# Rounded queries times key-value matrices, and three reordered steps, in a gated-linear and latent-attention block

## The chip, the cores and the metric

The kernel runs on one core of one Trainium2 chip. The metric is the device time of a whole execution in microseconds; lower is better. Times are medians of several executions, and one further execution is taken by the hardware profiler, whose rows are quoted here.

The core's engines run side by side, each with its own queue of instructions: TensorE (PE; its weight loads are listed as PEld), VectorE (DVE), ScalarE (ACT), GpSimd (POOL) and SyncE (SP), which here only issues transfers. They wait for each other through semaphores. TensorE accumulates into PSUM banks; all other working data lies in SBUF.

## The reference

One block on 512 tokens of width 1024, batch 1, in float32: an RMS norm, one wide input projection, two branches, a gated merge, an output projection, and an MLP with squared ReLU. Cut to what the change touches:

```python
def gla_direction(q, k, v, log_a, include_diag):       # per head; DK = 128, DV = 256
    b = jnp.cumsum(log_a, axis=3)
    q_dec = q * jnp.exp(b)
    k_dec = k * jnp.exp(-b)
    k_end = k * jnp.exp(b_last - b)
    scores = jnp.where(mask, einsum(q_dec, k_dec), 0.0)
    o_intra = einsum(scores, v)
    # over chunks:
    o = einsum('bhck,bhkv->bhcv', qc, state)
    state = state * dc[..., None] + einsum('bhck,bhcv->bhkv', kc, vc)

o = rmsnorm(o_f + o_b, g_gla) * silu(gr)               # four heads, forward and backward

q = rmsnorm(cq, g_q) @ w_uq                            # eight heads of the second branch
kv = rmsnorm(ckv, g_kv) @ w_ukv
k_rope = rope(kr, positions)                           # one rotary key for all heads
p = softmax(q k^T);  y_mla = p v

merged = sigmoid(z_ma) * y_gla + sigmoid(z_mb) * y_mla
h = h + merged @ w_out
h = h + square(relu(rmsnorm(h) @ w_ff1)) @ w_ff2
out = rmsnorm(h, g_final)
```

The gated-linear branch carries a key-value matrix, the state, of 128 by 256 for each head and direction. The kernel is free to choose how it chunks the sequence.

## The kernel before, in words

**Arithmetic.** Most float32 products are made of three rounded ones. A tensor x is kept as a pair: hi is x in the type fp32r (ScalarE writes it, `split`, L93), lo is x - hi, also in fp32r (a subtraction, L94, on VectorE, or on GpSimd where `split` is given that engine; `split_scaled`, L97 and L98, does the same with a factor). `mm3` (L87 to L90) then issues three matmuls into one accumulator: hi by hi (L88), hi by lo (L89), lo by hi (L90). Weights are loaded by SyncE into a staging tile and split; their tiles end in f, h and l (`gk2f`, `gk2h`, `gk2l`). Where both operands are left in plain float32, there is one `nc.tensor.matmul`, which the trace lists as two instructions.

**Stages.** (1) The input projection: blocks of it as one level of a seven-product scheme, the rest as 128 columns at a time against the split, transposed input `xT`. (2) The four heads of the gated-linear branch, from about 180 to 290 us, with the remaining input projections in between to fill TensorE. (3) The eight heads of the second branch ("the attention"), from about 296 us, as scores, softmax, transposes and values, with the up-projections of later heads and the first output-projection products in between. (4) The output projection and the MLP, in the seven-product scheme again.

**A head of the gated-linear branch**, in the loop of L1257 for heads 0 to 2 and written out from L1305 for the last. The 512 tokens are four blocks of 128, the state is taken over halves of 256. `Gates(h + 1)` (L441) makes the next head's decays: Abs, Exp and Ln on ScalarE (`logs`, L460), scans and differences on VectorE (`sums`, L463 to L476), exponentials (`exps`). `Scaled` multiplies queries and keys by them; `across` leaves in `far` (`qk3`) the queries (`far[:, 0]`) and keys (`far[:, 1]`) scaled to reach the other half of the sequence. `gla_scores` (L540) makes the scores inside a half (`sc`, split) and turns the far keys (`kT`, split). `gla_state` (L574) multiplies these by the values `v`, 24 rounded matmuls of 256 columns into one bank, and copies the bank to `gla{h}s`. `gla_out` (L727) accumulates into two banks: scores by values, 24 rounded matmuls, and then the far queries by the state of the other half, four plain float32 matmuls (L742). `gla_squares` and `gla_gated` (L763) norm and gate the result out of those two banks. Between state and output stand the weights' low part of the next projection (`lows`, L243) and other splits on VectorE.

**Around the last head.** Names that the steps touch: `rotary.tables` (L858; sine and cosine on ScalarE), `rotary_k` (L891 to L897; writes `krsin`, `kswap` and `kr` on VectorE), `ckv_.diagonals` (L811; the reciprocal norm of the key latent as a split diagonal `ckvdg`, L292) and `ckv_.spread` (L818, matmuls on L301 that spread it over the partitions), `rotary_begin` (L864; weights `wr0`, `wr1`) and `up_T` with them (`ro`), `rotary_q` (L878), `rotary_k_split` (`kbuf`), the gates `zb4` to `zb7` (`over_rms`, L375, then Tanh), and `up_units(0)`, the first pair of attention heads: queries `uq`, keys `uk`, values `uv`. `zb7` is the last projection before the attention; its weights are begun at L1330, its products run at L1338.

**Banks.** PSUM has eight banks in two rings of four: the tag "mm" (projections) and the tag "at" (scores, states, outputs, transposes). `ps(tag, name)` takes the next bank of its ring, and its first write waits until the bank's previous reader is done. `proj_begin(w, col, name, tag="mm")` (L231) loads, splits and takes a bank.

**Order.** Instructions of an engine keep the order in which they were issued. A scheduler may move them where the program doesn't fix it: `in_program_order(start, engines)` (L110) pins the named engines' order for the instructions since a mark, and `goes_behind` (L125) puts one group behind another. GpSimd is pinned to the program's order over all four heads (L1343), TensorE is up to L1341 (`ordered`, from the input projection on), and the attention is left to the scheduler but for the groups that `goes_behind` names.

Of the kernel before, what the change touches and what calls it, by code (L numbers as in the profile page):

```python
# [14 lines left out]
AF = mybir.ActivationFunctionType  # L15
# [3 lines left out]
P = 128  # L19
# [6 lines left out]
GH, GDV = 4, 256  # L26
# [9 lines left out]
C_ZA, C_ZB = 3776, 4800  # L36
# [20 lines left out]
def tile_block(ctx: ExitStack, tc: tile.TileContext, t, out: bass.AP):  # L57
    nc = tc.nc
# [5 lines left out]
    def tl(shape, dt, tag, bufs, name):  # L64
        serial[0] += 1
        return sb.tile(shape, dt, tag=tag, bufs=bufs, name=f"{name}_{serial[0]}")

    def u2(name, dt=F32, shape=(P, S)):
        return tl(list(shape), dt, "u2", 29, name)

    def u4(name, dt=F32R, shape=(P, 2, S)):
        return tl(list(shape), dt, "u4", 26, name)
# [14 lines left out]
    def mm3(acc, lh, ll, rh, rl, start, stop, onto=False):  # L87
        nc.tensor.matmul(acc, lh, rh, start=start, stop=False, skip_group_check=onto)  # L88
        nc.tensor.matmul(acc, lh, rl, start=False, stop=False, skip_group_check=onto)  # L89
        nc.tensor.matmul(acc, ll, rh, start=False, stop=stop, skip_group_check=onto)  # L90

    def split(hi, lo, src, rest=nc.vector):
        nc.scalar.activation(hi, src, AF.Copy)  # L93
        rest.tensor_tensor(lo, src, raw(hi), op=ALU.subtract)  # L94
# [134 lines left out]
    w_in = t["w_in"][0]  # L229

    def proj_begin(w, col, name, tag="mm"):  # L231
        wh, wl = weights(w[:, col : col + P], name)
        return wh, wl, ps(tag, name)
# [139 lines left out]
    def over_rms(acc, name):  # L373
        z = u2(f"z{name}")
        nc.vector.tensor_tensor(z, acc, R, op=ALU.mult)  # L375
        return z
# [163 lines left out]
    def gla_scores(near, nxt, far):  # L540


        bd = ps("at", "bd")
        for j in range(NT):
            nc.tensor.matmul(  # L545
                bd[:, j * P : (j + 1) * P], near["b"][:, 1, j], near["b"][:, 0, j], start=True, stop=True
            )
        scs = [ps("at", f"sc{g}") for g in range(2)]

        def block(j, i):  # L550
            at = (j % 2) * 256 + (i % 2) * P
            return scs[j // 2][:, at : at + P]

        for j in range(NT):
            n = j + 1 if j % 2 == 0 else j - 1
            nc.tensor.matmul(block(j, j), near["f"][:, 1, j], near["f"][:, 0, j], start=True, stop=True)
            nc.tensor.matmul(block(j, n), nxt[:, 1, j], nxt[:, 0, n], start=True, stop=True)
        kt = ps("at", "kt")
        for j in range(NT):
            nc.tensor.transpose(kt[:, j * P : (j + 1) * P], far[:, 1, j], ident)  # L560
        bds = u2("bds")
        nc.scalar.activation(bds, bd, AF.Copy)  # L562
        res = [u4(f"sc{g}") for g in range(2)]
        for g in range(2):
            for j in (2 * g, 2 * g + 1):
                nc.vector.copy_predicated(block(j, j), after.bitcast(I32), bds[:, j * P : (j + 1) * P])
            nc.scalar.activation(res[g][:, 0, :], scs[g], AF.Copy)
        for g in range(2):
            nc.vector.tensor_tensor(res[g][:, 1, :], scs[g], raw(res[g][:, 0, :]), op=ALU.subtract)
        keys = u4("kT")  # L570
        split(keys[:, 0, :], keys[:, 1, :], kt)
        return res, keys, far

    def gla_state(h, keys):  # L574

        half, at = h // 2, (h % 2) * GDV
        c = slice(at, at + GDV)
        acc = ps("at", f"gla{h}st")
        for j in range(NT):
            tok = slice(j * P, (j + 1) * P)  # L580
            mm3(acc[:, (j // 2) * GDV : (j // 2 + 1) * GDV], keys[:, 0, tok], keys[:, 1, tok],
                v[j, half][:, 0, c], v[j, half][:, 1, c], j % 2 == 0, j % 2 == 1)
        state = u2(f"gla{h}s")
        nc.scalar.activation(state, acc, AF.Copy)
        return state

# [138 lines left out]
    def gla_out(h, sc, state, far):  # L727

        half, at = h // 2, (h % 2) * GDV
        accs = [ps("at", f"gla{h}o{g}") for g in range(2)]  # L730
        c = slice(at, at + GDV)
        os = [accs[i // 2][:, (i % 2) * GDV : (i % 2 + 1) * GDV] for i in range(NT)]
        for i, o in enumerate(os):
            g = i // 2
            for x in range(2):
                j = 2 * g + x
                tok = slice(x * 256 + (i % 2) * P, x * 256 + (i % 2 + 1) * P)
                mm3(o, sc[g][:, 0, tok], sc[g][:, 1, tok], v[j, half][:, 0, c], v[j, half][:, 1, c],
                    i % 2 == 0 and x == 0, False, True)
        for i, o in enumerate(os):  # L740
            other = 1 - i // 2
            nc.tensor.matmul(  # L742
                o, far[:, 0, i], state[:, other * GDV : (other + 1) * GDV], start=False, stop=True,
                skip_group_check=True,
            )
        return os

    def gla_squares(h, os):
# [31 lines left out]
    class Latent:  # L780
# [4 lines left out]
        def begin(self, j):  # L785
            self.begun[j] = proj_begin(w_in, self.col + j * P, f"{self.name}{j}")
# [104 lines left out]
    def rotary_k():  # L891
        r = slice(64, 96)
        sgn = u2("krsin")
        nc.vector.tensor_scalar(sgn[r], sin[r], cst[r, K_SIGN : K_SIGN + 1], None, op0=ALU.mult)
        nc.vector.tensor_tensor(kswap[r], kswap[r], sgn[r], op=ALU.mult)
        nc.vector.tensor_tensor(kr[r], kr[r], cos[r], op=ALU.mult)
        nc.vector.tensor_tensor(kr[r], kr[r], kswap[r], op=ALU.add)  # L897
# [285 lines left out]
    ckv_, cq_ = Latent(C_CKV, 2, V_KV, "ckv"), Latent(C_CQ, 3, V_Q, "cq")  # L1183
# [7 lines left out]
    for n, (a, m) in enumerate(steps[:-4]):  # L1191
# [4 lines left out]
        if steps[n + 1] in fillers:  # L1196
            at = traced()
# [57 lines left out]
    rotary = Rotary()  # L1255
    pooled = traced()
    for h in range(GH - 1):  # L1257
        sc, keys, far = gla_scores(*scaled_qk.parts())
        scaled_qk = Scaled(h + 1)
        gate = Gates(h + 1)  # L1260
        gate.logs()
        latent, j = ((cq_, 1), (cq_, 2), (ckv_, 0))[h]
        acc = latent.products(j)
        if h < 2:
            w_b, lows = begin_late(C_GQ + (h + 2) * P, f"gq{h + 2}")
        else:
            ckv_.begun[1], lows = begin_late(C_CKV + P, "ckv1")
        (rotary.angles, rotary.reduced, cq_.diagonals)[h]()
        gate.sums("f")
        state = gla_state(h, keys)  # L1270
        gate.exps("f")
        lows()
        latent.keep(j, acc)
        gate.sums("b")
        gate.exps("b")
        scaled_qk.within("f", gate.parts)
        scaled_qk.across("f", gate.parts)
        if j:
            latent.add_squares()
        if h:  # L1280
            gla_turn(h - 1)
        os = gla_out(h, sc, state, far)
        scaled_qk.within("b", gate.parts)
        rs = gla_squares(h, os)
        scaled_qk.across("b", gate.parts)
        if h < 2:
            w_k = begin_qk(h + 2, 1)
            gla_gated(h, os, rs)
            finish_qk(h + 2, 0, w_b)
            if h == 0:  # L1290
                cq_.begin(2)
            else:
                ckv_.begin(0)
                cq_.sums()
            finish_qk(h + 2, 1, w_k)
        else:
            zb = begin(C_ZB + 4 * P, "zb4")
            gla_gated(h, os, rs)
            cq_.spread()
            ckv_.keep(1, ckv_.products(1))  # L1300
            ckv_.add_squares()
            w_b = begin(C_ZB + 5 * P, "zb5")
            zb = proj_run(zb, xT)

    h = GH - 1  # L1305
    sc, keys, far = gla_scores(*scaled_qk.parts())
    ckv_.sums()
    zb5 = proj_run(w_b, xT)
    cq = cq_.normed()
    state = gla_state(h, keys)  # L1310
    cos, sin = rotary.tables()
    late = [over_rms(acc, f"b{f}") for f, acc in ((4, zb), (5, zb5))]
    rotary_k()
    ckv_.diagonals()
    wr = rotary_begin()
    zb = begin(C_ZB + 6 * P, "zb6")
    kbuf = rotary_k_split()
# [9 lines left out]
    ro = rotary_q(accs)  # L1327
    zb = over_rms(proj_run(zb, xT), "b6")
    next(units)
    w_b = begin(C_ZB + 7 * P, "zb7")  # L1330
    g2.append(half_tanh(zb, "b6"))
    first_units = traced()
    for n, _ in enumerate(units):
# [3 lines left out]
    at = traced()  # L1337
# [20 lines left out]
    at = traced()  # L1358
# [4 lines left out]
    for n in range(4 * MH + LAG_C - 1):  # L1363
# [12 lines left out]
        if 2 <= n % 8 < 7:  # L1376
            at = traced()
# [5 lines left out]
        if n in (6, 14):  # L1383
            units = up_units(n // 8 + 2)
            at = traced()
# [3 lines left out]
        b = n - LAG_B  # L1389
        if n == 30:  # L1390
            xs_ = wo_accs[1] = [ps("mm", f"wox{rb}") for rb in range(2)]
            at = traced()
# [13 lines left out]
        for x, at in (("y", (18, 26, 34)), ("z", (20, 28, 36))):  # L1406
            if n in at:
                p = at.index(n)
                to = (5, 6) if x == "y" else (7, 3)
                split_sum(wo_left[p], sums_of[p, x], *to, f"{x}o{p}", nc.gpsimd if p < 2 else nc.vector)  # L1410
        if n in (19, 30):
            p = (19, 30).index(n)
# [12 lines left out]
        if n == 17:  # L1425
            at = traced()
# [235 lines left out]
    at = traced()  # L1662
# [9 lines left out]
    at = traced()  # L1672
# [7 lines left out]
    at = traced()  # L1680
# [12 lines left out]
    at = traced()  # L1693
# [8 lines left out]
    for qd in range(NQ):  # L1702
# [14 lines left out]
        for n, m in enumerate(ORDER):  # L1717
# [4 lines left out]
            if m == 2:  # L1722
                accs, begin = [ps("mm", f"gw{qd}{rb}") for rb in range(2)], True
# [3 lines left out]
            else:  # L1727
                accs, begin = (zs_, m == 5) if m in (5, 3) else (xs_, m == 1)
# [46 lines left out]
```

## Time and profile before

| | us |
|---|---|
| median of 3 runs | 755.55 |
| lowest and highest | 755.13, 756.49 |
| the profiled execution's own time | 754.4 |
| its span | 752.7 |
| mean granted TensorE clock, share of full speed | 0.997 |

Busy time by stretch of the span, us:

| stretch | length | PE | DVE | ACT | POOL | DMA share |
|---|---|---|---|---|---|---|
| 0 to 180, input projection | 180 | 178.46 | 146.62 | 115.08 | 48.73 | 0.61 |
| 180 to 270, heads 0 to 2 and the start of head 3 | 90 | 90.00 | 66.33 | 57.06 | 43.22 | 0.21 |
| 270 to 296, the rest of head 3 and the first pair | 26 | 24.45 | 21.52 | 17.09 | 8.94 | 0.50 |
| 296 to 480, attention and output projection | 184 | 183.94 | 153.80 | 133.28 | 52.94 | 0.57 |
| 480 to 753, MLP | 273 | 266.00 | 192.21 | 135.24 | 11.91 | 0.30 |

How rows are read. A row of the timeline gives start, duration, engine, line and operation, the tile written, the tiles read, the shape and type, and how many equal instructions follow each other; brackets at its end give how long the engine sat idle before it and what released it. A group row gives busy time and the mean duration in ns. A row of the waits names the waiting instruction, the one that released it, the total idle time, the number of times and the longest. Durations of matmuls overlap, because they are pipelined; the distance from start to start is what one costs.

### The profile page before, as it was taken

To read this page: it belongs to the slowest core of one execution; us is meant where nothing else is said; L and a number is where in the kernel's file an instruction comes from. 1 tells how busy PE (TensorE), PEld (TensorE's weight loads), DVE (VectorE), ACT (ScalarE), POOL (GpSimd) and SP (SyncE) were. 2 spreads that over 40 slices of the span, in tenths; PEclk is the share of its full clock that TensorE was granted. 3 is DMA by queue.
4 is the path that set the end of the run, shared out by engine and by line. 5 is a ranking of instruction groups with operands and counts; after the bars stand their busy time and mean duration, and the time that the engine had idled before them with its cause. 6 is when DMAs were issued, how large, how long until landed. Compare 5 with 4: busy or idle time off the path is not lost.

```text
span 752.7 us, 10206 instructions
## 1 busy us (share of the span) xinstructions
PE 742.9 (99%) x3688; PEld 628.0 (83%) x3688; DVE 580.5 (77%) x842; ACT 457.7 (61%) x776; POOL 165.7 (22%) x238
## 2 busy tenths in 40 slices
PE   9999999999999999999999999999999999999996
PEld 7888888888889888899988988888888888888885
DVE  7777886989787577888897688856696578748795
ACT  7557574686567476978865766345644465345644
POOL 0722110262573522246750100000000000000014
PEclk9999999999999999999999999999999999999998
DMA  9859582611322234458798321461126310650003
GB/s 310 263 124 241 168 175 82 113 29 32 80 57 39 39 85 108 110 146 220 222 194 256 115 66 44 154 182 56 57 80 199 115 56 15 198 152 0 29 0 112
DMA packets 94722, 88.90 MB, mean 118 GB/s; under 512 B 15792, under 2 KB 66992, under 8 KB 94672
## 3 DMA queue, kind: packets, MB, share of 16 engines
q1 hardware_dynamic: 88176, 75.64, 33.8%
q0 software_dynamic: 6208, 12.32, 9.3%
q8 instruction: 29, 0.48, 0.3%
q10 hardware_dynamic: 288, 0.28, 0.1%
q14 instruction: 21, 0.17, 0.1%
HBM read 83.25 MB, written 2.10 MB: 113 GB/s over the span
## 4 chain that ended last, share of the span: by engine, by line
PE 95%; DVE 2%; ACT 1%; issue 1%; POOL 0%; POOLq 0%; ACTq 0%
PE f L88 8%; PE f L89 8%; PE f L90 8%; PE gx L88 4%; PE gx L90 4%; PE gx L89 4%; PE first L330 3%; PE tp L1122 2%; PE gz L88 2%; PE gz L90 2%; PE gz L89 2%; PE zb L88 1%; PE zb L89 1%; PE zb L90 1%; PE av L88 1%; PE s L88 1%
## 5 line engine op out<-in xcount | busy, mean ns | idle before, releaser
L1714 POOL DMA_DIRECT2D gfin<-in_g_final x1 | 0.6, 628 | 283.9 <-PE f L90 283.9
L977 DVE TENSOR_TENSOR w<-w,w 128x1024 f32<-128x1024 f32 x32 | 38.7, 1220 | 0.3
L1102 DVE TENSOR_REDUCE top<-s 128x1 f32<-128x512 f32 x32 | 21.9, 684 | 3.6 <-PE s L90 3.0
L1107 ACT ACTIVATE e<-s,top 128x512 f32<-128x512 f32 x32 | 22.0, 688 | 3.5 <-DVE top L1102 3.4
L1452 DVE TENSOR_TENSOR h<-h,gx 128x512 f32<-128x512 f32 x32 | 21.5, 680 | 1.9 <-PE gx L90 1.8
L94 DVE TENSOR_TENSOR pT<-tp,pT 128x512 fp32r<-128x512 f32 x32 | 21.6, 681 | 1.5 <-ACT pT L93 1.5
L93 ACT ACTIVATE pT<-tp 128x512 fp32r<-128x512 f32 x32 | 18.9, 595 | 2.7 <-PE tp L1122 2.5
L1122 PE MATMUL tp<-ident,e 128*128 128x128 f32 x128 | 19.4, 274 | 0.0
L88 PE MATMUL av<-pT,v 128*128 128x256 f32 x64 | 19.1, 298 | 0.0
L93 ACT ACTIVATE ghb<-y 128x512 fp32r<-128x512 f32 x16 | 10.1, 632 | 14.0 <-DVE y L923 14.0
L1518 ACT ACTIVATE fa<-f 128x512 f32<-128x512 f32 x32 | 18.5, 577 | 0.0
L89 PE MATMUL av<-pT,v 128*128 128x256 f32 x64 | 18.2, 285 | 0.0
L90 PE MATMUL av<-pT,v 128*128 128x256 f32 x64 | 18.1, 283 | 0.0
L1122 PEld LDWEIGHTS tp<-ident,e 128*128 128x128 f32 x128 | 15.2, 140 | 3.3 <-ACT e L1113 0.4
L93 ACT ACTIVATE b_00h<-w 128x1024 fp32r<-128x1024 f32 x7 | 7.4, 1060 | 12.6 <-PE gz L90 6.0
L562 ACT ACTIVATE bds<-bd 128x512 f32<-128x512 f32 x4 | 2.4, 597 | 20.5 <-PE bd L545 20.5
L93 ACT ACTIVATE b_10h<-w 128x1024 fp32r<-128x1024 f32 x7 | 7.4, 1060 | 12.1 <-PE gz L90 6.0
L93 ACT ACTIVATE b_20h<-w 128x1024 fp32r<-128x1024 f32 x7 | 7.4, 1059 | 12.1 <-PE gz L90 6.0
L88 PE MATMUL s<-kbuf,q 96*128 96x512 f32 x32 | 14.1, 441 | 0.0
L1527 ACT ACTIVATE px<-fa 128x256 f32<-128x256 f32 x32 | 13.4, 418 | 1.0
L973 POOL DMA_DIRECT2D w<-in_w_out x10 | 12.3, 1406 | 7.6 <-DVE bo60l L94 6.5
L646 POOL DMA_DIRECT2D gvw<-in_w_in x4 | 4.8, 1226 | 38.7 <-DVE gvw L651 34.0
(1769 smaller groups left out, 2917.6 us busy)
## 6 DMA issues: line engine op xcount, KB each, us to landing
w<-in_w_ff SPq DMA_DIRECT2D x64, 256.0 KB, 3.5
w<-in_w_out POOLq DMA_DIRECT2D x10, 512.0 KB, 9.2
grw<-in_w_in SPq DMA_DIRECT2D x8, 512.0 KB, 8.6
zaw<-in_w_in SPq DMA_DIRECT2D x8, 512.0 KB, 7.3
gvw<-in_w_in SPq DMA_DIRECT2D x8, 512.0 KB, 4.5
w<-in_w_out SPq DMA_DIRECT2D x16, 256.0 KB, 5.3
x<-in_xt SPq DMA_DIRECT2D x8, 256.0 KB, 5.1
vw<-in_w_first SPq DMA_DIRECT2D x8, 256.0 KB, 5.3
```

Of the source, the lines that this page charges most:

```text
L88: nc.tensor.matmul(acc, lh, rh, start=start, stop=False, skip_group_check=onto)
L89: nc.tensor.matmul(acc, lh, rl, start=False, stop=False, skip_group_check=onto)
L90: nc.tensor.matmul(acc, ll, rh, start=False, stop=stop, skip_group_check=onto)
L93: nc.scalar.activation(hi, src, AF.Copy)
L94: rest.tensor_tensor(lo, src, raw(hi), op=ALU.subtract)
L330: nc.tensor.matmul(f_accs[i], a[:, i * P : (i + 1) * P], b, start=k == 0 and x == 0, stop=k == KD - 1 and x == 2)
L977: nc.vector.tensor_tensor(wq[dst][g], wq[x][g], wq[y][g], op=op)
L1102: nc.vector.tensor_reduce(top, acc, axis=AX.X, op=ALU.max, negate=True)
L1107: nc.scalar.activation(e, acc, AF.Exp, bias=top, accum_out=tot[:, qt % 2 : qt % 2 + 1])
L1122: nc.tensor.transpose(tp[:, k * P : (k + 1) * P], e[:, k * P : (k + 1) * P], ident)
L1452: nc.vector.tensor_tensor(hc, hc, acc, op=op)
L1518: nc.scalar.activation(a, acc, AF.Relu)
```

## The change

Four edits.

1. The state becomes a (hi, lo) pair: instead of one copy to float32, ScalarE writes hi and VectorE subtracts lo, both out of the state's bank.
2. The far queries become a pair as well: `far_queries` has ScalarE write hi and GpSimd subtract lo. It is called after `Gates(h + 1)` and ahead of `gate.logs()` in heads 0 to 2, and right after `gla_scores` in the last head.
3. The product of the two is `mm3`, twelve rounded matmuls of 256 columns in place of four plain float32 ones.
4. In the last head sine and cosine are issued ahead of the state, the key latent's diagonal ahead of the key rotation, and `zb7` takes its bank from the ring "at" instead of "mm".

```diff
@@ gla_state
-        state = u2(f"gla{h}s")
-        nc.scalar.activation(state, acc, AF.Copy)
+        state = u4(f"gla{h}s")
+        split(state[:, 0, :], state[:, 1, :], acc)
         return state
+
+    def far_queries(far):
+
+        hl = u4("qF")
+        split(hl[:, 0, :], hl[:, 1, :], far[:, 0].rearrange("p a b -> p (a b)"), nc.gpsimd)
+        return hl
@@ gla_out
         for i, o in enumerate(os):
-            other = 1 - i // 2
-            nc.tensor.matmul(
-                o, far[:, 0, i], state[:, other * GDV : (other + 1) * GDV], start=False, stop=True,
-                skip_group_check=True,
-            )
+            other = slice((1 - i // 2) * GDV, (2 - i // 2) * GDV)
+            tok = slice(i * P, (i + 1) * P)
+            mm3(o, far[:, 0, tok], far[:, 1, tok], state[:, 0, other], state[:, 1, other], False, True, True)
         return os
@@ heads 0 to 2
         gate = Gates(h + 1)
+        far = far_queries(far)
         gate.logs()
@@ the last head
     sc, keys, far = gla_scores(*scaled_qk.parts())
+    far = far_queries(far)
     ckv_.sums()
     zb5 = proj_run(w_b, xT)
     cq = cq_.normed()
+    cos, sin = rotary.tables()
     state = gla_state(h, keys)
-    cos, sin = rotary.tables()
     late = [over_rms(acc, f"b{f}") for f, acc in ((4, zb), (5, zb5))]
+    ckv_.diagonals()
     rotary_k()
-    ckv_.diagonals()
     wr = rotary_begin()
...
-    w_b = begin(C_ZB + 7 * P, "zb7")
+    w_b = proj_begin(w_in, C_ZB + 7 * P, "zb7", "at")
```

## The prediction, made before the changed kernel ran

> **What bounds the kernel now.** I read the busy times and the chain that ended last on the profile's page first, then TensorE's own waits.
>
> ```profile
> span 752.7 us, 10206 instructions
> PE 742.9 (99%) x3688; PEld 628.0 (83%) x3688; DVE 580.5 (77%) x842; ACT 457.7 (61%) x776; POOL 165.7 (22%) x238
> ...
> PE 95%; DVE 2%; ACT 1%; issue 1%; POOL 0%; POOLq 0%; ACTq 0%
> ```
> ```profile
> PE ckvrs L301 <- DVE ckvdg L292: 1.0, 1, 1.0
> PE zb L88 <- DVE q L98: 0.5, 1, 0.5
> ```
>
> TensorE is busy for 99% of the span and makes 95% of the last chain. Between the start and the end of the kernel it waits for others twice: 1.0 us for the key latent's diagonal, 0.5 us for a PSUM bank held by the first pair's queries. So the change can pay in two ways only: shorter work on TensorE, and these two waits. It costs nothing on another engine until an operand reaches TensorE late. The timeline shows how near each head is to that.
>
> **The far product on TensorE.** Rows of head 0 (start, duration):
>
> ```profile
> 184.41 0.28 PE L88 MATMUL gla0o<-gv,sc 128*128 128x256 f32 x1
> 184.53 0.28 PE L89 MATMUL gla0o<-gv,sc 128*128 128x256 f32 x1
> ...
> 187.30 1.89 PE L742 MATMUL gla0o<-gla0s,qk 128*128 128x256 f32 x8
> ...
> 189.25 0.39 PE L89 MATMUL gq<-xT,gq2h 128*128 128x512 f32 x1
> ...
> 194.74 0.39 PE L89 MATMUL gk<-xT,gk2h 128*128 128x512 f32 x1
> 194.96 0.39 PE L90 MATMUL gk<-xT,gk2l 128*128 128x512 f32 x1
> ```
>
> Durations overlap, so I go by starts. A rounded matmul of 256 columns starts 0.12 us after the one before, one of 512 columns 0.23 us. Now: the eight plain f32 instructions of L742 plus one gq matmul take 189.25 - 187.30 = 1.95 us. Then: 12 x 0.12 + 0.23 = 1.67 us. That saves **0.29 us a head, 1.16 us in four**, where TensorE does not wait for operands.
>
> **What the operands cost.** Each head gains a ScalarE copy (queries, hi), a GpSimd subtraction (queries, lo) and a VectorE subtraction from PSUM (state, lo). ScalarE's copy of the state only changes its form. In the changed program's order the queries' hi stands on ScalarE ahead of the Ln table load, and the state's lo on VectorE between the forward difference and the next weights' low part.
>
> ```profile
> 182.18 1.06 ACT L460 ACTIVATE l<-l 128x1024 f32<-128x1024 f32 x1
> 191.30 1.09 ACT L93 ACTIVATE gk2h<-gk2f 128x1024 fp32r<-128x1024 f32 x1
> ...
> 374.67 0.62 ACT L93 ACTIVATE ghyo<-yo 128x512 fp32r<-128x512 f32 x1
> 375.19 0.62 ACT L93 ACTIVATE ghzo<-zo 128x512 fp32r<-128x512 f32 x1
> ```
> ```profile
> 183.34 1.37 DVE L468 TENSOR_TENSOR_SCAN rrf<-mf,l 128x128 f32<-128x128 f32 x4
> 185.35 1.22 DVE L243 TENSOR_TENSOR gq2l<-gq2f,gq2h 128x1024 fp32r<-128x1024 f32 x1
> 192.42 1.51 DVE L94 TENSOR_TENSOR gk2l<-gk2f,gk2h 128x1024 fp32r<-128x1024 f32 x1 [0.76 <-ACT gk2h L93]
> 264.43 1.28 DVE L375 TENSOR_TENSOR zb<-zb,R 128x512 f32<-128x512 f32 x2
> ```
> ```profile
> L94 POOL TENSOR_TENSOR glyo<-yo,ghyo 128x512 fp32r<-128x512 f32 x2 | 2.6, 1290 | 0.9 <-PE tp L1122 0.5 <-ACT ghyo L93 0.4
> ```
>
> A copy of this size takes 0.52 us from start to start (374.67 to 375.19). The scan starts at 183.34, 0.10 us after Ln ends (182.18 + 1.06), so it moves by the whole 0.52. The state's lo takes 0.60 us (two operations of that shape out of PSUM in 1.28, the second 0.68 long). Behind these two stand the backward scan, the exponentials, the squares, and gk2h with gk2l. All slide by **1.12 us**. The GpSimd subtraction takes about 1.29 us and falls at 181.5 to 182.8; far lo is wanted near 187. I cost it at nothing; without that cover it would cost up to its 1.29 a head.
>
> State lo then ends near 186.6 and is wanted at 187.42: hidden. What is late next is gk2l. It ended at 193.93; now 195.05. TensorE's L90, 0.29 us earlier, would start at 194.67, and its weights load one matmul ahead. From the end of gk2l I allow 0.06 us for the signal and 0.12 for the load: 195.2. **Stall 0.53 us in head 0**. The bounds are 0 (if the 1.51 shrinks to gq2l's 1.22 and the slide is a little less) and 0.85.
>
> ```profile
> 219.59 1.47 DVE L94 TENSOR_TENSOR gk3l<-gk3f,gk3h 128x1024 fp32r<-128x1024 f32 x1 [1.94 <-ACT gk3h L93]
> 247.44 1.22 DVE L94 TENSOR_TENSOR zb4l<-zb4f,zb4h 128x1024 fp32r<-128x1024 f32 x1 [2.58 <-ACT zb4h L93]
> ```
> ```profile
> 222.76 0.40 PE L90 MATMUL gk<-xT,gk3l 128*128 128x512 f32 x1
> 250.14 0.39 PE L90 MATMUL zb<-xT,zb4l 128*128 128x512 f32 x1
> ```
>
> Head 1: 221.06 + 1.12 + 0.18 = 222.36 against 222.47: 0 (up to 0.4). Head 2: 248.66 + 1.30 = 249.96 against 249.85: 0.11 (0 to 0.5). Three heads save 0.87 and give back 0.64: **-0.2 us** at the last head's start.
>
> **The last head's order.** Sine and cosine move ahead of the state's copy on ScalarE, the diagonal ahead of the key rotation on VectorE.
>
> ```profile
> 266.29 0.60 ACT L584 ACTIVATE gla3s<-gla3st 128x512 f32<-128x512 f32 x1 [2.92 <-PE gla3st L90]
> 271.42 0.62 ACT L93 ACTIVATE kbuf<-kr 32x512 fp32r<-32x512 f32 x1 [0.19 <-DVE kr L897]
> ```
> ```profile
> 268.87 0.48 DVE L894 TENSOR_SCALAR krsin<-sin,gvec 32x512 f32<-32x512 f32 x1 [3.15 <-ACT sin L860]
> 271.41 0.16 DVE L812 TENSOR_TENSOR ckvr<-ckvr,r_x 128x4 f32<-128x4 f32 x1
> 273.10 0.55 DVE L94 TENSOR_TENSOR wr0l<-wr0f,wr0h 128x384 fp32r<-128x384 f32 x1
> 286.57 1.21 DVE L94 TENSOR_TENSOR zb7l<-zb7f,zb7h 128x1024 fp32r<-128x1024 f32 x1
> 292.01 0.88 DVE L763 SCALAR_TENSOR_TENSOR grb<-gla3o,gla3ss,grb 128x256 f32<-128x256 f32 x2
> ```
> ```profile
> 269.78 1.89 PE L742 MATMUL gla3o<-gla3s,qk 128*128 128x256 f32 x8
> 272.63 1.10 PE L301 MATMUL ckvrs<-ckvdg,ones_r 128*128 128x512 f32 x2 [0.97 <-DVE ckvdg L292]
> 274.05 0.40 PE L90 MATMUL ro<-cqhl,wr0l 128*128 128x512 f32 x1
> 290.07 0.47 PE L88 MATMUL zb<-xT,zb7h 128*128 128x512 f32 x1 [0.48 <-DVE q L98]
> 290.61 0.40 PE L90 MATMUL zb<-xT,zb7l 128*128 128x512 f32 x1
> 296.31 0.40 PE L88 MATMUL s<-kbuf,q 96*128 96x512 f32 x1
> ```
>
> Taken alone the spread would start at 269.78 + 1.44 = 271.22 instead of 272.63. But VectorE's new first step, the state's lo, waits for the state: hi ends at 266.89, lo runs 266.93 to 267.53 by starts, the two zb scalings (moved behind it) to 268.75. Then the diagonal group takes 273.10 - 271.41 = 1.69, to 270.44: in time, the 0.97 is gone. The rotation (271.41 - 268.87 = 2.54) now stands between the diagonal and wr0l, which starts at 272.98 and ends at 273.53. With 0.18 us its L90 starts at 273.7; it was 274.05. Unhindered it would have been 271.2 + 0.5 (spread) + 0.5 = 272.2. So the wait of L301 goes, a wait of about 1.5 us at wr0l comes: **gain here 0.3 us**, bounds 0 and 1.8.
>
> The rotation ends at 272.98 instead of 271.41, so ScalarE's kbuf, the Tanh table load behind it, the squares and the latent's split all slide by 1.6 us, and everything on VectorE from there to zb7l and the gating.
>
> **The last gate's bank.** With a bank of the other kind zb7 no longer waits for q: 0.5 us idle and 0.1 of pickup go, and L88 could start at 289.1. zb7l ends at 287.78 + 1.6 = 289.38; L90 is wanted near 289.6: stall 0 to 0.1. So **0.6 us** is gained. In exchange the second score block takes a bank of the last head's output and waits for the first two gatings. They end at 292.89 + 1.6 = 294.5; the block starts at 296.31 - 1.1 = 295.2: free by 0.7 us.
>
> In the attention the changed program holds the same matmuls with as many changes between transposes and rounded products (33), in a slightly different order. I cost that at 0, between -0.5 and +0.7 us (32 steps of 0.02, a tenth of a 512-column matmul).
>
> **Sum:** -0.2 - 0.3 - 0.6 = **-1.1 us**. The profiled execution took 754.4 us (its span and 1.7 us around it), 1.15 us under the median of the runs, 755.55. So 753.3 by the profile, and **754.4 us** for the median.
>
> **Rivals.**
>
> 1. *All operands come in time.* For it: ScalarE is busy for only 61%, and the low parts miss by half a microsecond in one head. Against it: wr0l misses by 1.5. Gain 1.16 + 0.97 + 0.5 for the second half of the spread and pickup + 0.6 = 3.2: 752.3 us.
>
> 2. *The heads give everything back.* The slide is 1.5 rather than 1.12 us, with a miss in each of three heads (0.9, 0.3, 0.5) and nothing gained at wr0l: -0.87 + 1.7 - 0.6 = +0.2: 755.8 us.
>
> 3. *Slower: zb7l becomes the bound.* VectorE and GpSimd hinder each other where both read SBUF.
>
> ```profile
> 280.19 0.97 DVE L885 TENSOR_TENSOR roa<-roa,rob 128x512 f32<-128x512 f32 x1
> 283.96 0.69 DVE L885 TENSOR_TENSOR roa<-roa,rob 128x512 f32<-128x512 f32 x1
> ```
> ```profile
> 280.15 3.18 POOL L94 TENSOR_TENSOR wk0l<-wk0f,wk0h 128x128 fp32r<-128x128 f32 x4 [0.16 <-ACT wk0h L93]
> ```
>
> The same operation takes 0.28 us more while GpSimd splits wk0. If the slid rotation of the queries waits out all of wk0l, zb7l ends 3.2 us later still, at 292.6, and from 289.4 on each microsecond is TensorE's: -1.1 + 3.2 = +2.1: 757.6 us. Against it: the one overlap shown costs 0.28.
> [...]
>
> **How the numbers follow.** Chances: forecast 0.45, all in time 0.18, heads give back 0.19, slower 0.18. A measurement of this kernel can tell about 0.2%, 1.5 us, from no change. The forecast's own range by its bounds is 753.2 to 755.4, so a third of its chance lies beyond -1.5 us. Faster 0.18 + 0.15 = 0.33, put at 0.36 for the near misses; slower 0.18; within 0.46. The range leaves out the far end of either side: 752.2 to 757.2.
>
> **What would show it.** Right: L742's twelve successors start 0.12 us apart; a TensorE wait on gk2l of about 0.5 us in head 0; no wait at ckvrs, but one of 1 to 2 us at ro's first L90 for wr0l; zb7 starting right behind uv; the second block of scores about 1.1 us earlier than 296.31, at 295.2, and the same offset at the end. Wrong: the far products more than 0.14 us apart, wr0l in time, zb7l later than 290, or waits of over 0.3 us in the attention.

## The result, and the profile after

| | before | changed |
|---|---|---|
| median of 16 runs, us | 755.16 | 756.59 |
| lowest and highest | 754.23, 756.96 | 756.16, 757.29 |
| the profiled execution, us | 754.4 | 756.17 |
| its span | 752.7 | 754.4 |

The change made the kernel slower: the ratio is 1.0021, its 95% interval 1.0014 to 1.0028. Forecast were 754.4 us, 1.1 us faster, and a range up to 757.2; the time fell into the range, on the other side of no change.

The lines of the changed kernel's profile page that answer to those of before, the span, the busy times and the shares of the last chain by engine:

```profile
span 754.4 us, 10247 instructions
PE 741.8 (98%) x3704; PEld 627.8 (83%) x3704; DVE 587.6 (78%) x846; ACT 459.8 (61%) x780; POOL 168.9 (22%) x242
...
PE 94%; DVE 3%; ACT 1%; issue 1%; POOL 0%; POOLq 0%; ACTq 0%; DVEq 0%
```

TensorE is busy 1.1 us less (742.9 before), and the span is 1.7 us longer: the products did become shorter, and more than that was lost in waits. TensorE's own waits in the changed kernel (who waits, for whom, total us, times, longest):

```profile
PE ro L90 <- DVE wr0l L94: 1.7, 1, 1.7
...
PE ro L88 <- ACT yg L780: 1.2, 1, 1.2
PE av L88 <- DVE tb L1154: 0.9, 1, 0.9
PE gk L90 <- DVE gk2l L94: 0.6, 1, 0.6
```

The two waits of before, for ckvdg and for q, are both gone, as forecast. Four others stand in their place. The view counts idle time alone; from start to start, beyond the usual distance of two matmuls, the four cost 1.86, 1.37, 1.03 and 0.74 us, and some 0.1 us more where the weight loads restart: behind wr0l the delayed matmul is listed with 0.50 us instead of 0.40 and the next starts 0.34 after it instead of 0.23 (274.37 to 274.71).

Where the time went is read from first starts in the timeline of TensorE, here the changed kernel:

```profile
187.48 0.28 PE L88 MATMUL gla0o<-gla0s,qF 128*128 128x256 f32 x1
...
188.92 0.40 PE L88 MATMUL gq<-xT,gq2h 128*128 128x512 f32 x1
...
264.98 0.28 PE L88 MATMUL gla3st<-gv,kT 128*128 128x256 f32 x1
...
285.09 0.39 PE L88 MATMUL uq<-cqhl,wq0h 128*128 128x512 f32 x1
...
291.37 0.40 PE L88 MATMUL zb<-xT,zb7h 128*128 128x512 f32 x1
...
296.83 0.40 PE L88 MATMUL s<-kbuf,q 96*128 96x512 f32 x1
...
367.57 0.40 PE L88 MATMUL wox<-bo10h,gao 128*128 128x512 f32 x1
...
380.23 0.40 PE L88 MATMUL wox<-bo11h,gao 128*128 128x512 f32 x1
```

| first start of | before | changed | later by | in this stage | forecast for the stage |
|---|---|---|---|---|---|
| bd, head 0's first product | 173.93 | 174.11 | 0.18 | (nothing changed yet) | 0 |
| gla3st, the last head's state | 264.60 | 264.98 | 0.38 | +0.20 | -0.2 |
| uq, first pair of the attention | 283.16 | 285.09 | 1.93 | +1.55 | -0.3 |
| s, first scores | 295.62 | 296.83 | 1.21 | -0.72 | -0.6 |
| wox, first output products | 366.68 | 367.57 | 0.89 | -0.32 | 0 |
| wox after the last values | 378.49 | 380.23 | 1.74 | +0.85 | 0 |

From there to the end 0.06 us comes back. Profiles start with an offset that has nothing to do with the change (up to 1.2 us at bd among the runs below), so what is read from traces below is taken from bd on.

### The profile page after: what moved, and what is told of

Read it like the earlier page. It is cut to its first block, busy times and chain, and to the rows that moved or that the text cites. A ratio compares the mean times of both kernels' runs of the same rounds, so it can differ in the third digit from the quotient of the medians.

```text
span 754.4 us, 10247 instructions
## 1 busy us (share of the span) xinstructions
PE 741.8 (98%) x3704; PEld 627.8 (83%) x3704; DVE 587.6 (78%) x846; ACT 459.8 (61%) x780; POOL 168.9 (22%) x242
## 4 chain that ended last, share of the span: by engine, by line
PE 94%; DVE 3%; ACT 1%; issue 1%; POOL 0%; POOLq 0%; ACTq 0%; DVEq 0%
PE f L88 8%; PE f L89 8%; PE f L90 8%; PE gx L88 4%; PE gx L89 4%; PE gx L90 4%; PE first L330 3%; PE gz L89 2%; PE gz L88 2%; PE gz L90 2%; PE tp L1126 2%; PE zb L88 1%; PE zb L89 1%; PE zb L90 1%; PE s L88 1%; PE s L89 1%
## 5 line engine op out<-in xcount | busy, mean ns | idle before, releaser
L90 PE MATMUL av<-pT,v 128*128 128x256 f32 x64 | 18.2, 284 | 0.0
```

## The experiments

Each set shares its runs of the kernel before: 755.10 us for the first four, 754.87 for the second, 755.01 for the third. Medians of 5 or 11 runs. In the run with both waits removed and in the four that move the state's low part, the order of VectorE and ScalarE in the last head is pinned to the program's, which their rows in the changed kernel follow without it. Single runs of one kernel lie up to 2.8 us apart, so differences under half a microsecond are read from the traces.

### The three parts alone

**The far product and its splits alone** (the order of the last head and zb7's bank put back):

```diff
-    cos, sin = rotary.tables()
     state = gla_state(h, keys)
+    cos, sin = rotary.tables()
...
-    ckv_.diagonals()
     rotary_k()
+    ckv_.diagonals()
...
-    w_b = proj_begin(w_in, C_ZB + 7 * P, "zb7", "at")
+    w_b = begin(C_ZB + 7 * P, "zb7")
```

> Only the far product and its two splits; the last head keeps the old order and zb7 its old bank, and the attention is in the order of before. My theory: heads 0 to 2 lose 0.2 us net as in the changed kernel (gk2l waits about 0.8, gk3l 0.25), and in the last head the state's lo on VectorE (0.6 us) pushes the diagonal back by as much, so the wait of ckvrs grows from 1.1 to about 2.0 us and eats the 0.3 of the shorter product: about +0.8 us, 756.0. Rival (the far product pays for itself and the loss is all from the reordering): -0.2 us or better, at most 755.0.

Measured: 755.75 us, ratio 1.0011 (1.0002 to 1.0019). The heads lose 0.26 us by the trace. The wait at ckvrs grows only from 1.0 to 1.2 us (idle), where about 2.0 were expected; most of the rest is lost at zb7, whose wait for q grows from 0.5 to 1.1. The rounded far product doesn't pay for itself, even in the old order.

**The order of sine and diagonal alone**, on the kernel before:

```diff
+    cos, sin = rotary.tables()
     state = gla_state(h, keys)
-    cos, sin = rotary.tables()
...
+    ckv_.diagonals()
     rotary_k()
-    ckv_.diagonals()
```

> Only sine and diagonal moved, with the plain float32 far product and the old bank. My theory: without the state's lo on VectorE the diagonal is ready near 267.5 us and the rotation ends near 270, so wr0l comes in time and the 1.6 us of waits at ckvrs go: about -1.5 us, 753.7, with no wait at wr0l or wr1h over 0.2. Rival (the reordering itself costs: the rotation ahead of wr0l makes TensorE wait there whatever the far product does): a wait of 1 to 2 us at wr0l or at wr1h and a total between -0.3 and +1.5.

Measured: 753.58 us, ratio 0.9977 (0.9968 to 0.9986). TensorE's waits after the start are down to one:

```profile
PE zb L88 <- DVE q L98: 0.5, 1, 0.5
```

So the reordering itself is good for 1.5 us, and the rotation ahead of wr0l costs nothing there.

**The bank of zb7 alone**, on the kernel before:

```diff
-    w_b = begin(C_ZB + 7 * P, "zb7")
+    w_b = proj_begin(w_in, C_ZB + 7 * P, "zb7", "at")
```

> Only zb7's bank. Its order in the attention is that of the changed kernel. My theory: zb7 starts 0.6 to 0.7 us earlier, and the attention's new order keeps or gains 0.3 up to the first output products; the last values wait 0.2 us, or up to 1.0 if the wait behind VectorE's subtraction of glyo (0.68 before, 1.23 us after) comes with the new order: 754.2 to 755.0. Rival (the new order itself costs): the gain at zb7 is given back and the total is +0.2 us or more, above 755.3.

Measured: 754.81 us, ratio 0.9998 (0.9989 to 1.0007). By the trace 0.74 us are gained up to the first scores and 0.33 up to the output products, and 0.85 are lost at a wait that the kernel before does not list:

```profile
PE av L88 <- DVE tb L1150: 0.9, 1, 0.9
```

The three parts alone make +0.65, -1.52 and -0.29 us, together -1.16. That this is close to the forecast of -1.1 is chance: the forecast's terms were -0.2 for the heads, -0.3 for the last head and -0.6 for the bank, and no part alone made its term. All at once they made +1.43. So 2.6 us are an interaction, and the next runs look for its place. By the first starts it has two parts: +3.2 us up to uq, where the changed kernel has the waits for wr0l and yg that none of the three has alone, and -0.7 us at zb7, where the far product alone adds 0.6 to the wait for q and the new bank takes that wait away. The order of instructions on each engine shows that of the three the bank is what changes the order in the attention; the other two parts leave it as it was.

### What the last head waits for

**The two copies yg ahead of kbuf**, in the changed kernel:

```diff
+    gla_turn(h - 1)
     kbuf = rotary_k_split()
     g2 += [half_tanh(z, f"b{f}") for f, z in ((4, late[0]), (5, late[1]))]
-    gla_turn(h - 1)
```

> The changed kernel with the two copies yg of the third head's transposes ahead of kbuf and the Tanh table load on ScalarE. My theory: wr1h's wait of 1.4 us is for the bank that yg frees; yg then runs near 269.4 to 270.6 and the wait goes, so the last head ends about 1.4 us earlier: 755.2 to 755.5, with the wait at wr0l (1.9 us) unchanged. Rival (wr1h waits for something else that comes as late, or zb7l then makes TensorE wait as long): within 0.3 us of the changed kernel, 756.3 to 756.9.

Measured: 755.52 us, ratio to before 1.0004 (0.9995 to 1.0013), 1.1 us under the changed kernel, at the edge of what was expected. The wait for yg is gone from the list; those for wr0l (1.7), tb (0.9) and gk2l (0.6) stand unchanged. The changed kernel's ScalarE and TensorE rows show the chain:

```profile
273.76 0.63 ACT L93 ACTIVATE kbuf<-kr 32x512 fp32r<-32x512 f32 x1 [4.40 <-DVE kr L901]
274.40 1.28 ACT L380 ACT_TABLE_LOAD   x1
275.70 1.15 ACT L380 ACTIVATE tb<-zb 128x512 f32<-128x512 f32 x2
276.75 1.25 ACT L780 ACTIVATE yg<-y,gla_gain 128x512 f32<-128x512 f32 x2
```
```profile
274.37 0.50 PE L90 MATMUL ro<-cqhl,wr0l 128*128 128x512 f32 x1 [1.69 <-DVE wr0l L94]
...
277.48 0.50 PE L88 MATMUL ro<-cqhl,wr1h 128*128 128x512 f32 x1 [1.20 <-ACT yg L780]
```

ScalarE sat idle for 4.40 us in front of kbuf. Behind kbuf, the table load and the two Tanh stood yg, whose input was there: in this run, placed ahead of kbuf, it starts at 269.57. wr1h's product takes the PSUM bank in which the third head's transposes lay, and yg is the reader that frees it. In the kernel before, yg stood in the same place on ScalarE, 2.2 us earlier without the offset:

```profile
274.41 1.25 ACT L776 ACTIVATE yg<-y,gla_gain 128x512 f32<-128x512 f32 x2
```

**Both waits removed, with the rotation behind wr0l and wr1l**, in the changed kernel with yg ahead of kbuf:

```diff
     ckv_.diagonals()
-    rotary_k()
     wr = rotary_begin()
+    rotary_k()
```

> The changed kernel with wr0l and wr1l ahead of the key rotation on VectorE and the copies yg ahead of kbuf on ScalarE; nothing else moves. My theory: both waits of the last head go (1.9 at wr0l, 1.4 at wr1h), TensorE reaches zb7 3.4 us earlier, but VectorE's chain from the latent's low part through the rotation of the queries to zb7l (ready at 290.0 in the changed kernel) does not come earlier, so zb7's first L90 waits 1.5 to 1.9 us for it: 1.6 to 2.0 us under the changed kernel, 754.6 to 755.0. Rival (VectorE's chain follows TensorE): no wait at zb7l over 0.3, and 753.2 to 753.5.

Measured: 755.34 us, ratio 1.0006 (0.9997 to 1.0015). TensorE's waits:

```profile
PE uk L88 <- DVE roa L887: 1.3, 1, 1.3
PE av L88 <- DVE tb L1154: 0.9, 1, 0.9
PE gk L90 <- DVE gk2l L94: 0.6, 1, 0.6
PE uv L88 <- DVE zb L375: 0.2, 1, 0.2
```

The waits for wr0l and yg went, and uk waits 1.3 us; the total is 0.3 us above the expected span. That VectorE's chain does not come earlier was right; the place was wrong. The row names the rotation of the queries: VectorE's last read of the first ro bank releases uk, well ahead of zb7l. Pushing work back on VectorE only moved the wait.

**The state's low part behind the diagonal**, one instruction moved in the changed kernel (the two helper lines keep the split's second half until then):

```diff
-    state = gla_state(h, keys)
+    state = gla_state(h, keys, later)
     late = [over_rms(acc, f"b{f}") for f, acc in ((4, zb), (5, zb5))]
     ckv_.diagonals()
+    later[0]()
     rotary_k()
```

> The changed kernel with one instruction moved: in the last head the state's low part stands on VectorE behind the diagonal instead of ahead of the two gate scalings. My theory: VectorE stood idle 1.93 us there, waiting for the state's high part with the scalings, the diagonal, the rotation and wr0l ready behind it; all of them now come 1.9 us earlier, the wait at wr0l falls from 1.9 to 0.2 or less, the wait at wr1h stays at 1.2 to 1.5 (its bank comes 1.9 earlier too): 754.5 to 755.0. Rival (the rotation ahead of wr0l costs by itself, wherever the state's low part stands): wait at wr0l over 1 us, 756.0 to 756.8.

Measured: 754.69 us, ratio 0.9994 (0.9985 to 1.0003), 1.9 us under the changed kernel. VectorE in the changed kernel:

```profile
263.81 1.88 DVE L832 TENSOR_TENSOR cqhl<-cqc,cqhl 128x512 fp32r<-128x512 f32 x3
267.62 0.69 DVE L94 TENSOR_TENSOR gla3s<-gla3st,gla3s 128x512 fp32r<-128x512 f32 x1 [1.93 <-ACT gla3s L93]
268.23 1.28 DVE L375 TENSOR_TENSOR zb<-zb,R 128x512 f32<-128x512 f32 x2
...
273.76 0.56 DVE L94 TENSOR_TENSOR wr0l<-wr0f,wr0h 128x384 fp32r<-128x384 f32 x1
```

and in this one:

```profile
263.84 1.88 DVE L837 TENSOR_TENSOR cqhl<-cqc,cqhl 128x512 fp32r<-128x512 f32 x3
265.65 1.27 DVE L375 TENSOR_TENSOR zb<-zb,R 128x512 f32<-128x512 f32 x2
...
268.52 0.68 DVE L588 TENSOR_TENSOR gla3s<-gla3st,gla3s 128x512 fp32r<-128x512 f32 x1
...
271.78 0.56 DVE L94 TENSOR_TENSOR wr0l<-wr0f,wr0h 128x384 fp32r<-128x384 f32 x1
```

The 1.93 us of idle time in brackets are gone, everything behind comes 1.98 earlier, and wr0l ends at 272.34, in time for its L90 at 272.55. The wait for yg stays, at 1.2. This is the larger part of the interaction. The far product alone has such a wait too, as its VectorE rows show:

```profile
267.23 0.69 DVE L94 TENSOR_TENSOR gla3s<-gla3st,gla3s 128x512 fp32r<-128x512 f32 x1 [1.54 <-ACT gla3s L93]
...
269.17 0.48 DVE L898 TENSOR_SCALAR krsin<-sin,gvec 32x512 f32<-32x512 f32 x1
```

There it costs little: in the old order the key rotation comes next, which needs sine, and sine ends only at 269.14. In the new order sine and cosine are done before the state's copy, so the diagonal and the rotation are ready and the wait pushes all of them; that the copy now stands behind sine and cosine adds the last 0.4 of the 1.93 us. The order alone, without a subtraction, lets the rotation start early:

```profile
262.68 1.89 DVE L828 TENSOR_TENSOR cqhl<-cqc,cqhl 128x512 fp32r<-128x512 f32 x3
...
267.48 0.48 DVE L894 TENSOR_SCALAR krsin<-sin,gvec 32x512 f32<-32x512 f32 x1
```

In the changed kernel krsin starts at 271.21, 3.6 us later without the offset: 1.0 by which VectorE already reaches cqhl later (the slide of the heads), 1.93 of idle time and 0.6 for the subtraction itself. The other two, 1.6 us, are then what is left behind the wait for yg, which stays when the idle time goes; this is worked out from the rows, and no run took them apart.

### The heads

**The queries' low part on VectorE**, the far product alone, in heads 0 to 2:

```diff
-        far = far_queries(far)
+        qf, far = far, u4("qF")
+        nc.scalar.activation(far[:, 0, :], qf[:, 0].rearrange("p a b -> p (a b)"), AF.Copy)
         gate.logs()
...
+        nc.vector.tensor_tensor(far[:, 1, :], qf[:, 0].rearrange("p a b -> p (a b)"), raw(far[:, 0, :]), op=ALU.subtract)
         gate.sums("f")
```

> The far product alone, as in the run before, with the low part of the far queries in heads 0 to 2 on VectorE, right ahead of the scan, instead of on GpSimd. My theory: GpSimd's subtraction (1.31 us) held up VectorE's turns (0.43 before, 1.39 after) and with them the scan; on VectorE it falls into the wait for Ln, turns takes 0.43 again, the scan starts 0.3 us earlier and the wait at gk2l falls from 0.75 to about 0.45; with head 1 that makes 0.3 to 0.5 less than the far product alone: 755.2 to 755.5. Rival (the slide is that of Ln and the state's lo alone, and another operation on VectorE only adds to it): wait at gk2l 0.75 or more, 755.7 to 756.3.

Measured: 755.33 us, ratio 1.0001 (0.9993 to 1.0010), 0.4 us under the far product alone, within the noise of that difference. The traces decide: gk2l's wait falls from 0.75 to 0.38 by starts, gk3l's goes, and the heads gain 0.38 us where they had lost 0.26. VectorE in the kernel before, VectorE and GpSimd in the changed kernel, then VectorE in this run:

```profile
181.66 0.43 DVE L846 TENSOR_SCALAR turns<-ang 128x512 f32<-128x512 f32 x1
```
```profile
181.84 1.39 DVE L850 TENSOR_SCALAR turns<-ang 128x512 f32<-128x512 f32 x1
...
184.34 1.37 DVE L468 TENSOR_TENSOR_SCAN rrf<-mf,l 128x128 f32<-128x128 f32 x4
```
```profile
181.64 1.31 POOL L94 TENSOR_TENSOR qF<-qk,qF 128x512 fp32r<-128x512 f32 x1 [9.82 <-ACT qF L93]
```
```profile
182.04 0.43 DVE L850 TENSOR_SCALAR turns<-ang 128x512 f32<-128x512 f32 x1
...
184.17 1.37 DVE L468 TENSOR_TENSOR_SCAN rrf<-mf,l 128x128 f32<-128x128 f32 x4
```

turns began 0.20 us after GpSimd's subtraction and ended 0.28 after it: it waited the other out. An engine that looked free, at 22%, cost the busy one 0.96 us. (The offset of this trace is 0.2 larger.)

### The wait before the last values

**The merge tb ahead of glyo** on VectorE, with zb7's bank alone (the split of y moves behind the last head's values, n is 35):

```diff
-        for x, at in (("y", (18, 26, 34)), ("z", (20, 28, 36))):
+        for x, at in (("y", (18, 26)), ("z", (20, 28, 36))):
...
+            valued = traced()
             att_values(c // 4, (c % 4) // 2)
+            valued = valued, traced()
+        if n == 35:
+            at = traced()
+            split_sum(wo_left[2], sums_of[2, "y"], 5, 6, "yo2", nc.vector)
+            goes_behind((at, traced()), valued, SPLITTERS[1:])
```

> zb7's bank alone, as in the run before, with the merge of the last head's first half (tb) ahead of glyo on VectorE. My theory: the 1.03 us that TensorE waits before the last values is the wait for tb, which stands behind a glyo that GpSimd's sum (my) holds back from 0.68 to 1.23 us; the wait falls to 0.2 or less and the total by 0.8 to 1.0 against the bank alone: 753.8 to 754.1. Rival (the last values wait for something else, or glyo then comes late for the output products): 754.5 to 755.1.

Measured: 755.16 us, ratio 1.0000 (0.9992 to 1.0009): a miss. By the trace the wait for tb is gone and TensorE is 1.1 us earlier than with the bank alone at the next products, but 0.78 us of that is lost again by the end, most of it at one wait:

```profile
PE wox L88 <- ACT f00h L93: 0.4, 1, 0.4
```

So tb was the cause of the 1.0. The next wait is put down to ScalarE's f00h, a split of later weights that the waiting product does not read; what really holds it back was not pursued. VectorE and GpSimd at the wait, in the changed kernel:

```profile
376.31 0.78 DVE L94 TENSOR_TENSOR gao<-mx,gao 128x512 fp32r<-128x512 f32 x1
377.02 1.23 DVE L94 TENSOR_TENSOR glyo<-yo,ghyo 128x512 fp32r<-128x512 f32 x1
378.17 0.41 DVE L1154 SCALAR_TENSOR_TENSOR tb<-tb,av 128x256 f32<-128x256 f32 x1
```
```profile
375.80 0.74 POOL L1157 TENSOR_TENSOR mx<-tb,yg 128x256 f32<-128x256 f32 x1 [1.71 <-DVE tb L1154]
376.50 1.20 POOL L1157 TENSOR_TENSOR my<-tb,yg 128x256 f32<-128x256 f32 x1
```

and in the kernel before, where glyo came first:

```profile
375.82 0.68 DVE L94 TENSOR_TENSOR glyo<-yo,ghyo 128x512 fp32r<-128x512 f32 x1
```
```profile
375.87 1.22 POOL L1153 TENSOR_TENSOR my<-tb,yg 128x256 f32<-128x256 f32 x1
```

In the changed order gao holds my back to about 377.0, my then holds glyo back, and glyo holds tb; before, glyo began 0.05 us ahead of my and took its normal 0.68. That this is the reason for the longer glyo is read from these rows; no run took my away. The run with tb ahead of glyo agrees, for there glyo begins when less of my is left:

```profile
375.43 0.90 DVE L94 TENSOR_TENSOR glyo<-yo,ghyo 128x512 fp32r<-128x512 f32 x1
```
```profile
374.58 1.19 POOL L1153 TENSOR_TENSOR my<-tb,yg 128x256 f32<-128x256 f32 x1
```

### Versions put together

**Order, bank and tb, with the plain far product:**

> Sine and diagonal moved, zb7's bank, and tb ahead of glyo, with the plain float32 far product. My theory: without the far pair the other gains add up: -1.5 (order), -0.7 (zb7), -0.3 (attention's order) with no wait of 1.0 before the last values: 752.3 to 752.8. Rival (the gains overlap, zb7l or the first pair's operands make TensorE wait once it is 2.2 us early): 753.2 to 754.0, with a wait of 0.5 or more at zb7l or in the first pair.

Measured: 753.41 us, ratio 0.9974 (0.9965 to 0.9983): slower than expected, though not by a wait at zb7l or in the first pair. By the trace the gains do add up, to 2.9 us after the last values, and 0.8 go again, with the wait put down to f00h as above (0.3 here).

**The far pair with its three repairs** (run f2_three: state's low part behind the diagonal, yg ahead of kbuf, the queries' low part on VectorE):

> The same with the copies yg ahead of kbuf on ScalarE and the low part of the far queries in heads 0 to 2 on VectorE ahead of the scan. My theory: against the changed kernel 1.9 at wr0l, 1.5 at wr1h and 0.6 in the heads go, and VectorE's chain is now early enough for the key latent: 752.2 to 753.0, with no wait over 0.5 between 190 and 370 us. Rival (the wait moves on to the key latent, 1.5 us there as with the rotation behind wr0l): 753.5 to 754.3.

Measured: 752.17 us, ratio 0.9962 (0.9947 to 0.9976), 4.4 us under the changed kernel. Its waits:

```profile
PE av L88 <- DVE tb L1159: 0.9, 1, 0.9
PE gk L90 <- DVE gk2l L94: 0.2, 1, 0.2
```

(The rival's "key latent" is the wait of uk, which the row further up put down to ro's bank.)

**The same, with gk2h and gk3h ahead of the squares:**

```diff
+        if h < 2:
+            w_k = begin_qk(h + 2, 1)
         rs = gla_squares(h, os)
         scaled_qk.across("b", gate.parts)
         if h < 2:
-            w_k = begin_qk(h + 2, 1)
             gla_gated(h, os, rs)
```

> The same as f2_three with gk2h and gk3h ahead of the squares on ScalarE. My theory: gk2l is late only because gk2h stands behind the four squares; its wait (0.4) goes and the total falls by 0.3 to 0.5 against that run. Rival (gk2l waits for VectorE's own chain, or the squares then come late for the gating): the same as f2_three within 0.15 by the trace.

Measured: 751.85 us, ratio 0.9954 (0.9941 to 0.9967), the lowest median of all: 3.2 us under the kernel before. The wait for gk2l is gone; by the trace this is 0.6 us under the run above.

**f2_three with tb ahead of glyo:**

> The same as f2_three with tb ahead of glyo on VectorE. My theory: the 1.0 us wait before the last values goes, and 0.5 to 0.7 of it comes back at the last block of the output projection (bo40h with gdo), as with the bank alone: 0.3 to 0.6 less than f2_three. Rival (given back whole): within 0.15 of it by the trace.

Measured: 752.45 us, ratio 0.9960 (0.9947 to 0.9973), not told apart from f2_three by its time; by the trace 0.27 us less, just under the expected span. The wait for tb goes and that for f00h (0.4) comes, as with the bank alone. Against the run with order, bank and tb but the plain far product, the trace is 0.6 us shorter: with its operands well placed the rounded far product does pay, about half of the 1.16 us worked out for it.

## Why the prediction was wrong, step by step

**The far product's size: right.** Forecast 0.29 us a head (1.95 less 1.67 is 0.28). From the last product ahead of it to the second gq matmul head 0 gained 0.28 us, and its twelve rounded matmuls start 0.12 us apart (187.48 to 188.92).

**"I cost it at nothing" (GpSimd's subtraction): wrong.** The cover that I named was GpSimd's idleness and the late need of its result. But it stood in VectorE's way: turns 0.43 became 1.39, and the scan slid by 0.82 instead of 0.52 us (184.34 less 183.34, less the offset 0.18). gk2l's wait was 0.85 with its restart where 0.53 were forecast, gk3l's 0.27 where 0 were. The heads made +0.2 instead of -0.2. The overlap that I held against rival 3 (0.97 against 0.69) was misread: the row of wk0l holds four instructions, and the one that the rotation met takes 0.46 us. In the four overlaps read here, what an instruction lost went with how much of the other one was left when it started: turns lost 0.96 us with 1.11 of the subtraction left, glyo 0.55 with 0.68 of my left and 0.22 with 0.34 left, the rotation 0.28 with 0.42 left. Taken by single instructions, each lost what was left to within 0.15 us. That the rotation waits out all of wk0l, the 3.2 us of rival 3, no run shows: it lost 0.28 us in the kernel before and 0.14 in the changed one (0.83 less 0.69).

**"A wait of about 1.5 us at wr0l": right in kind, 0.3 short.** Besides the 0.2 us that the heads had lost, the state's high part ended 0.3 us later than worked out, because sine and cosine, now ahead of it on ScalarE, were not done earlier (it begins at 267.01, in the far product alone at 266.60). So the rotation and wr0l came later too; the wait was 1.86 by starts.

**"ScalarE's kbuf, the Tanh table load behind it, the squares and the latent's split all slide by 1.6 us": the step that failed most.** It was true, and I priced the slide at its far end (zb7l) alone. Between the Tanh and the squares stands yg, which frees the bank of the second ro product: 1.37 us of waiting, 1.48 with the restart. With the 0.3 above and 0.1 for wr0l's own restart, that is, within 0.1 us, the whole difference between the forecast -0.3 and the measured +1.55 in the last head.

**The same step named the cause and passed over it.** "VectorE's new first step, the state's lo, waits for the state" was written down as an order and not as idle time: 1.93 us with nothing running and the two gate scalings and the diagonal ready behind it. The run with the state's low part behind the diagonal shows its worth, 1.9 us for moving one instruction.

**zb7's bank: right,** 0.72 us against 0.6; zb7l came in time, and the third rival with it did not happen.

**The attention "at 0, between -0.5 and +0.7": inside its bounds** at +0.53, for a reason that it did not contain. I counted changes between kinds of matmul; by the rows around glyo what decided was the order of VectorE and GpSimd. That the total lies inside 752.2 to 757.2 is the width of that range and says nothing for the account.

Of the rivals, "the heads give everything back" comes nearest with its 755.8 us, and its slide of 1.5 us is near the 1.4 that VectorE shows in head 0 (gq2l at 186.95, before at 185.35, less the offset), but it placed the loss in the wrong stage.

## What to carry to other kernels

An instruction that waits at the head of an engine's line delays all the ready work behind it (here by 1.93 us), and costs little only where that work would have waited anyway (1.54 us in the far product alone, where sine was still to come); when a split is added, look first for the place in the line where its source has already arrived. When a slide of an engine is worked out, every instruction in it has to be asked whose PSUM bank it frees, not only whose operand it makes (here yg, 1.37 us). Parts that gain or lose alone say little about their sum: here +0.65, -1.52 and -0.29 us made +1.43, and with three edits of order and engine the same parts made -2.8.

## What the runs showed of the hardware

A GpSimd subtraction of 128 by 512 elements stopped a VectorE operation with a single SBUF input (turns, 0.43 us alone) for as long as it ran on: 1.39 us where it was overlapped, 0.43 again where the subtraction was on VectorE. Between operations with two SBUF inputs on both engines the order of starts went with which was stretched: glyo took 0.68 us where it began 0.05 us ahead of GpSimd's sum, and 1.23 where it began 0.52 behind it. In the four overlaps read here VectorE's operation lost what was left of GpSimd's when it began, less 0.12 to 0.15 us. The other way round, GpSimd's 128 by 4 subtraction v3f took 1.19 us in the kernel before, where it began 0.09 us behind VectorE's gq2l (185.44 and 185.35), and 0.20 in the changed kernel, where it began 0.09 behind VectorE's subtraction of the state (186.44 and 186.35), one of whose inputs is a PSUM bank.
